# A causal mask taken from TensorE's accumulation to an add on VectorE, in the softmax heads of a decoder trunk

## The chip, the core and the metric

The kernel runs on one core of a Trainium2 chip. The metric is device time in microseconds, the median of several runs. The engines are named as the profile does: PE is TensorE's matmul and PEld its weight load, DVE is VectorE, ACT is ScalarE, POOL is GpSimd, SP is SyncE. Matmuls accumulate in PSUM, which has eight banks of 128 partitions by 512 float32 values; the other engines read the results from there.

## The reference

The program is a two-layer decoder trunk on 512 tokens of width 1024: an attention layer with an MLP, then a gated short convolution with an MLP. The attention layer has eight softmax heads with a forget gate ("forgetting attention") and eight stick-breaking heads, each 64 wide. The change is in the softmax heads alone:

```python
logits = jnp.einsum('bhqd,bhkd->bhqk', qi, k) * scale
logits = logits + fi[..., :, None] - cum_f[:, :, None, :]
causal = key_pos[None, :] <= q_pos[:, None]
logits = jnp.where(causal, logits, -jnp.inf)
p = jax.nn.softmax(logits, axis=-1)
return jnp.einsum('bhqk,bhkd->bhqd', p.astype(v.dtype), v)
```

For a block of 128 queries, keys of earlier blocks are all seen, keys of later blocks are not computed, and only the 128x128 block on the diagonal needs a mask.

## The kernel before

**Tiles.** Attention goes by pairs of heads `p`: 0 to 3 are softmax heads, 4 to 7 stick-breaking ones. The two heads of a pair are `e` = 0 and 1; they lie on different halves of the 128 partitions. Within a pair there are three units `u`: query blocks 0 and 1 together, block 2, block 3. One unit of one head fills one PSUM bank with scores: queries on the partitions, keys along the row. In u=0 the bank holds block 0 (one key block, at column 0) and block 1 (two key blocks, at column 256).

**A unit.** `logits(p, u)` makes the scores by products of float32 values split into a high and a low half (`q_hi`, `q_lo`, `k_hi`, `k_lo`): three matmuls per block and head, and in softmax heads a fourth for the forget gate (`dl`, `dr`), all at L688. Then come the mask products at L697: an identity in bf16 as weights and `mask` (0 on and below the diagonal, -1e30 above) as the moving side, which add the mask to the diagonal block. VectorE takes the negated maximum of a row (L705, `top`), ScalarE the exponential and its sum (L706, `w`, `total`), VectorE the reciprocal (L708, `inv`) and the scaling (L711).

**Around it.** `turn` transposes the weights of the unit before on TensorE (L748 for blocks 0 and 1, L760 for 2 and 3) into a `psc` bank, from where ScalarE copies the high half and VectorE subtracts the low half (`pt`, L754/L755 and L763/L764). `weigh` multiplies by the values (L784), whose halves VectorE adds up (L791). Between these, TensorE works off projections for later pairs: queries and keys (L313, L314, L315), values (L570 to L572), the sums of squares of the norm of queries and keys (L607, turned at L615, read by VectorE at L617), and the rows of that norm (L640, multiplied at L642, split at L415/L416). Weights of projections are halved by ScalarE (L292, `whi`) and VectorE (L293, `wlo`). Stick-breaking units have sigmoids (L726, L727) and a scan (L729) in place of maximum and exponential, and no mask product.

**PSUM.** Banks are handed out in three groups: `psa` (2), `psb` (4) and `psc` (2). Scores and projections take `psb`, so a unit's scores may have to wait until the exponentials of an earlier unit have read their bank. Transposes, sums of squares and rows take `psc`, so they wait until VectorE and ScalarE have read what stood there.

**The order.** The code is written in an order set by a counter, `spend` (L215): `logits`, `turn` and the projections each add an estimate in microseconds, and `fill` works off projections until a quota is used up. For a softmax unit the estimate at L681 has 0.12 per block for the mask. A scheduler then orders each engine's instructions once more when the program is built, except where `keep_in_program_order` holds them. Each engine runs its own list strictly in order, and waits on semaphores of the others.

## Time and profile before

| | |
|---|---|
| median of 3 runs | 1127.98 us (1127.93 to 1128.21) |
| the profiled execution | 1127.62 us |
| its span | 1125.3 us |
| PE busy | 1115.6 us, 99% of the span |
| PEld busy | 1009.8 us, 90% |
| DVE busy | 943.4 us, 84% |
| ACT busy | 679.9 us, 60% |
| mask products (L697) | 32, from 52.4 to 141.8 us |
| maxima (L705) | 32, from 52.7 to 143.3 us |

The span is from the first to the last instruction of the execution; what is left of its time lies around that. A matmul's duration in the profile includes its way through a pipeline, so that matmuls overlap: how long one holds TensorE is read from the start of one to the start of the next. The granted TensorE clock is 1.00 throughout the softmax stage. A row of the timeline gives start, length, engine, line, operation, `out<-in`, shapes and a count of equal instructions that follow each other; in brackets stands the idle time before it and what ended that. A row of waits gives total, times and longest. A row of instructions by group gives total busy time and the mean duration in ns of one.

### The profile page before, as it was taken

Reading aid. Unit: us, or ns where it says so; the run is one execution under the profiler, and the core shown is the slowest. Engines: PE = TensorE matmul, PEld = TensorE weight load, DVE = VectorE, ACT = ScalarE, POOL = GpSimd, SP = SyncE. Lnnn points to the kernel's source line nnn. Section 1 sums busy time; section 2 is a strip of 40 time slices with the busy share of each in tenths; the row PEclk is TensorE's granted clock in tenths of the full one; section 3 lists DMA queues with packets and bytes.
Section 4 is the critical chain, followed back from the end, with each engine's and each line's share of the span. In section 5 each row is a group of like instructions: output and inputs, shape, how many; then the busy total and the mean of one; then the engine's idle time right before and its main releaser. Section 6 shows DMA issues by size and latency. Waiting matters only on the chain.

```text
span 1125.3 us, 19407 instructions
## 1 busy us (share of the span) xinstructions
PE 1115.6 (99%) x7691; PEld 1009.8 (90%) x7691; DVE 943.4 (84%) x1439; ACT 679.9 (60%) x1013; POOL 158.6 (14%) x191
## 2 busy tenths in 40 slices
PE   9999999999999999999999999999999999999998
PEld 7888787878899999999999899988889999998886
DVE  6787888887899787888989889875799888898886
ACT  7556676655466766666557455543456766677553
POOL 4011111111101110014400001111111110014300
PEclk9999999999999999999999999999999999999999
DMA  6678777687877777799963455798887766699951
GB/s 194 173 180 200 179 180 200 155 205 206 197 208 201 208 192 197 206 277 205 228 173 77 120 153 125 157 229 216 207 208 188 177 174 159 183 265 195 233 153 57
DMA packets 175690, 209.34 MB, mean 186 GB/s; under 512 B 7564, under 2 KB 140220, under 8 KB 175600
## 3 DMA queue, kind: packets, MB, share of 16 engines
q0 software_dynamic: 41024, 86.95, 39.1%
q1 hardware_dynamic: 134416, 121.09, 34.8%
q8 instruction: 60, 0.98, 0.4%
q14 instruction: 30, 0.25, 0.1%
q10 hardware_dynamic: 160, 0.07, 0.0%
HBM read 203.10 MB, written 49.28 MB: 224 GB/s over the span
## 4 chain that ended last, share of the span: by engine, by line
PE 90%; DVE 4%; issue 2%; DMA 2%; ACT 1%; SPq 0%; DVEq 0%; ACTq 0%; POOLq 0%
PE psb L1056 25%; PE psb L1602 11%; PE psa L1056 10%; PE psa L1602 8%; PE psb L313 5%; PE psb L315 5%; PE psb L314 5%; PE psa L315 3%; PE psa L313 3%; PE psa L314 3%; PE psa L784 2%; PE psb L688 2%; DMA Xc<-in_conv_w_in 2%; PE psb L570 1%; PE psc L315 1%
## 5 line engine op out<-in xcount | busy, mean ns | idle before, releaser
L292 ACT ACTIVATE whi<-raw 128x1024 fp32r<-128x1024 f32 (+2 forms) x89 | 91.7, 1031 | 93.6 <-PE psb L314 29.9
L293 DVE TENSOR_TENSOR wlo<-raw,whi 128x1024 fp32r<-128x1024 f32 (+2 forms) x89 | 105.5, 1185 | 24.2 <-ACT whi L292 23.2
L1056 PE MATMUL psb<-p_lo,whi_p 128*128 128x256 f32 x432 | 121.7, 282 | 0.0
L1056 PE MATMUL psb<-p_hi,wlo_p 128*128 128x256 f32 x432 | 121.6, 281 | 0.0
L1056 PE MATMUL psb<-p_hi,whi_p 128*128 128x256 f32 x432 | 121.4, 281 | 0.0
L313 PE MATMUL psb<-hs_a,whi 128*128 128x512 f32 x224 | 92.2, 412 | 0.0
L315 PE MATMUL psb<-hs_a,wlo 128*128 128x512 f32 x224 | 88.7, 396 | 0.0
L1056 PEld LDWEIGHTS psb<-p_hi,whi_p 128*128 128x128 f32 x432 | 81.9, 190 | 0.0
L1056 PEld LDWEIGHTS psb<-p_lo,whi_p 128*128 128x128 f32 x432 | 81.4, 188 | 0.0
L1056 PE MATMUL psa<-p_hi,wlo_p 128*128 128x256 f32 x288 | 81.2, 282 | 0.0
L1056 PEld LDWEIGHTS psb<-p_hi,wlo_p 128*128 128x128 f32 x432 | 81.2, 188 | 0.0
L1056 PE MATMUL psb<-q_lo,whi_q 128*128 128x256 f32 x288 | 81.1, 282 | 0.0
L1056 PE MATMUL psa<-p_lo,whi_p 128*128 128x256 f32 x288 | 81.1, 282 | 0.0
L1056 PE MATMUL psb<-q_hi,wlo_q 128*128 128x256 f32 x288 | 81.1, 281 | 0.0
L1056 PE MATMUL psa<-p_hi,whi_p 128*128 128x256 f32 x288 | 80.9, 281 | 0.0
L1056 PE MATMUL psb<-q_hi,whi_q 128*128 128x256 f32 x288 | 80.9, 281 | 0.0
L1602 PE MATMUL psb<-act,whi 128*128 128x256 f32 x352 | 63.2, 282 | 0.0
L423 DVE SCALAR_TENSOR_TENSOR uv<-yv,taps,uv 128x511 f32<-128x511 f32 (+1 forms) x80 | 56.6, 744 | 0.0
L1602 PE MATMUL psb<-whi,act 128*128 128x512 f32 x176 | 56.4, 398 | 0.0
L423 DVE SCALAR_TENSOR_TENSOR ug<-yg,taps,ug 128x511 f32<-128x511 f32 (+1 forms) x80 | 55.5, 744 | 0.0
L1056 PEld LDWEIGHTS psa<-p_hi,whi_p 128*128 128x128 f32 x288 | 54.5, 189 | 0.1
L1056 PEld LDWEIGHTS psb<-q_hi,whi_q 128*128 128x128 f32 x288 | 54.6, 189 | 0.0
(478 smaller groups left out, 3619.3 us busy)
## 6 DMA issues: line engine op xcount, KB each, us to landing
t<-in_ffn_w_up POOLq DMA_DIRECT2D x42, 768.0 KB, 8.0
t<-t POOLq DMA_DIRECT2D x18, 768.0 KB, 5.5
raw<-in_attn_w_in SPq DMA_DIRECT2D x24, 512.0 KB, 5.3
X<-in_ffn_w_up SPq DMA_DIRECT2D x18, 512.0 KB, 5.1
Y<-t SPq DMA_DIRECT2D x18, 512.0 KB, 6.6
three<-t SPq DMA_DIRECT2D x18, 512.0 KB, 3.7
W<-in_ffn_w_up SPq DMA_DIRECT2D x18, 512.0 KB, 4.0
X<-in_ffn_w_up POOLq DMA_DIRECT2D x18, 512.0 KB, 8.0
```

The source lines that it names most:

```text
L292: return (act.activation(hi[:, at_], raw[:, at_], AF.Copy), dve.tensor_tensor(lo[:, at_], raw[:, at_], f32(hi[:, at_]), op=ALU.subtract))
L293: dve.tensor_tensor(lo[:, at_], raw[:, at_], f32(hi[:, at_]), op=ALU.subtract))
L313: made = [pe.matmul(acc, w[0], rhs[0], start=first, stop=False), pe.matmul(acc, w[0], rhs[1], start=False, stop=False), pe.matmul(acc, w[1 ...
L314: pe.matmul(acc, w[0], rhs[1], start=False, stop=False),
L315: pe.matmul(acc, w[1], rhs[0], start=False, stop=last)]
L423: dve.scalar_tensor_tensor(dst[:, d:], src[:, 0:S - d], tap(j), dst[:, d:], op0=ALU.mult, op1=ALU.add)
L570: pe.matmul(acc, lhs[0], w[0], start=first, stop=False)
L688: pe.matmul(ss[e][:, c:c + wide], ql[rows, b * P:n], kl[rows, 0:wide], start=first and b == bs[0], stop=last and b == bs[-1])
L784: pe.matmul(out_, w, t[:, first:first + step * (NB - k - 1) + 1:step, :], start=k == 0 and i == 0, stop=k == NB - 1 and i == 1)
L1056: pe.matmul(to, w[a][:, k, c], x[b][:, k, :], start=fresh and i + k + t == 0, stop=i == 1 and k == 3 and t == 2, skip_group_check=not fresh)
L1602: pe.matmul(to, l, r, start=begin and o + t == 0, stop=end and t == 2 and o == (0 if layer else 1), skip_group_check=not fresh)
```

## The change

The 32 mask products leave TensorE's accumulation, and the scores of the forget gate become the last of the group. Instead VectorE adds `mask` in place to the diagonal blocks in the score bank, just before the first maximum of each head of a unit. In u=0 one instruction takes both diagonal blocks of a bank (columns 0 and 384, 128x2x128), in u=1 and u=2 it takes one (128x128): six per pair, 24 in all. L681 and all else in the code stay as they are.

```diff
         scores(q_lo, k_hi, False, not fox)
         if fox:
-            scores(dl[:, p, :], dr, False, False)
-            for e in range(2):
-                for b, n, c, _ in parts:
-                    pe.matmul(ss[e][:, c + b * P:c + n], ident16, mask, start=False, stop=b == bs[-1])
+            scores(dl[:, p, :], dr, False, True)
...
             for j, (b, n, c, a) in enumerate(parts):
                 for e in range(2):
+                    if j == 0:
+                        diag = ss[e].rearrange("p (k q) -> p k q", q=P)[:, bs[0]:NB:3, :]
+                        dve.tensor_tensor(diag, diag, mask[:, None, :].to_broadcast([P, m, P]), op=ALU.add)
                     dve.reduce_max(top[:, j, e:e + 1], ss[e][:, c:c + n], axis=AX.X, negate=True)
```

In the changed file the add is at L704; the maximum stays at L705. The scheduler orders TensorE, VectorE and ScalarE anew around the softmax units. Behind the last of them the three lists are the same as before, and those of GpSimd and SyncE are the same throughout. Three places follow; the numbers in names are those of tiles and differ between the two programs.

TensorE at p=0, u=1 (two score banks, one per head; `psb_730` is a projection's). Before:

```order
L615 MATMUL psc_750<-ident,flat_759 128x128 x2
L688 MATMUL psb_806<-qk_hi_643,qk_hi_654 128x384
L688 MATMUL psb_806<-qk_lo_644,qk_hi_654 128x384
L688 MATMUL psb_807<-qk_hi_643,qk_hi_654 128x384
L688 MATMUL psb_807<-qk_lo_644,qk_hi_654 128x384
L688 MATMUL psb_806<-qk_hi_643,qk_lo_655 128x384
L688 MATMUL psb_807<-qk_hi_643,qk_lo_655 128x384
L688 MATMUL psb_806<-dr,dl 128x384
L688 MATMUL psb_807<-dr,dl 128x384
L697 LDWEIGHTS begin
L697 MATMUL psb_806<-mask,begin 128x128
```

And in the changed program:

```order
L615 MATMUL psc_750<-ident,flat_759 128x128 x2
L688 MATMUL psb_804<-qk_hi_643,qk_hi_654 128x384
L688 MATMUL psb_804<-qk_lo_644,qk_hi_654 128x384
L688 MATMUL psb_804<-qk_hi_643,qk_lo_655 128x384
L688 MATMUL psb_804<-dr,dl 128x384
L313 MATMUL psb_730<-hs_a_119,whi_618 128x512
L314 MATMUL psb_730<-hs_b_120,whi_618 128x512
L688 MATMUL psb_805<-qk_hi_643,qk_hi_654 128x384
L688 MATMUL psb_805<-qk_lo_644,qk_hi_654 128x384
L688 MATMUL psb_805<-qk_hi_643,qk_lo_655 128x384
L688 MATMUL psb_805<-dr,dl 128x384
```

The two heads' scores, mixed before, stand apart now, with two projection matmuls between them.

TensorE at p=1, u=0, where the sums of squares of a later pair (L607) meet the scores. Before:

```order
L572 MATMUL psb_989<-whi_881,hs_b_120 128x256
L688 MATMUL psb_1013<-qk_hi_948,qk_hi_959 128x256
L688 MATMUL psb_1014<-qk_hi_948,qk_hi_959 128x256
L688 MATMUL psb_1013<-qk_hi_948,qk_hi_959 128x256
L688 MATMUL psb_1014<-qk_hi_948,qk_hi_959 128x256
L688 MATMUL psb_1013<-qk_lo_949,qk_hi_959 128x256
L688 MATMUL psb_1014<-qk_lo_949,qk_hi_959 128x256
L607 MATMUL psc_1015<-sq_876,head_ones 32x128 x4
L607 MATMUL psc_1015<-sq_978,head_ones 32x128 x4
L688 MATMUL psb_1013<-qk_lo_949,qk_hi_959 128x256
```

And in the changed program:

```order
L572 MATMUL psb_987<-whi_879,hs_b_120 128x256
L607 MATMUL psc_1013<-sq_874,head_ones 32x128 x4
L607 MATMUL psc_1013<-sq_976,head_ones 32x128 x4
L688 MATMUL psb_1011<-qk_hi_946,qk_hi_957 128x256
L688 MATMUL psb_1012<-qk_hi_946,qk_hi_957 128x256
L688 MATMUL psb_1011<-qk_hi_946,qk_hi_957 128x256
```

The sums of squares stood inside the scores and now stand ahead of all of them.

VectorE at p=3, u=0, behind the split of a query tile (L655) and with the low halves of the transposed weights of p=2, u=2 (L764). Before:

```order
L655 SCALAR_TENSOR_TENSOR qk_lo_1729<-psb_1620,head_gains,qk_hi_1728 128x512
L293 TENSOR_TENSOR wlo_1736<-raw_1737,whi_1735 128x1024
L705 TENSOR_REDUCE top_1707<-psb_1684 128x1
L705 TENSOR_REDUCE top_1707<-psb_1685 128x1
L705 TENSOR_REDUCE top_1707<-psb_1684 128x1
L705 TENSOR_REDUCE top_1707<-psb_1685 128x1
L764 TENSOR_TENSOR pt_1532<-psc_1747,pt_1531 128x512
L708 RECIPROCAL inv_1709<-total_1708 128x4
```

And in the changed program:

```order
L655 SCALAR_TENSOR_TENSOR qk_lo_1721<-psb_1614,head_gains,qk_hi_1720 128x512
L704 TENSOR_TENSOR psb_1678<-psb_1678,mask 128x2x128
L704 TENSOR_TENSOR psb_1679<-psb_1679,mask 128x2x128
L705 TENSOR_REDUCE top_1697<-psb_1678 128x1
L705 TENSOR_REDUCE top_1697<-psb_1679 128x1
L293 TENSOR_TENSOR wlo_1728<-raw_1729,whi_1727 128x1024
L705 TENSOR_REDUCE top_1697<-psb_1678 128x1
L705 TENSOR_REDUCE top_1697<-psb_1679 128x1
L764 TENSOR_TENSOR pt_1526<-psc_1739,pt_1525 128x512
L764 TENSOR_TENSOR pt_1526<-psc_1746,pt_1525 128x512
```

The adds and the first maxima stand ahead of the halving of projection weights (L293), and the second L764 ahead of the reciprocal. On TensorE the sums of squares that follow there (L607, at 128.5 us in the profile before) stand three projection matmuls later than before.

## The prediction

> **What bounds the kernel now.** I read the page first: span, busy shares, chain that ended last.
>
> ```profile
> span 1125.3 us, 19407 instructions
> PE 1115.6 (99%) x7691; PEld 1009.8 (90%) x7691; DVE 943.4 (84%) x1439; ACT 679.9 (60%) x1013; POOL 158.6 (14%) x191
> PE 90%; DVE 4%; issue 2%; DMA 2%; ACT 1%; SPq 0%; DVEq 0%; ACTq 0%; POOLq 0%
> ```
>
> TensorE is the bound: 90% of the chain. So the unit of account is TensorE's time. What it saves in the softmax stage reaches the end unless a later wait eats it; what VectorE gains or loses counts only where TensorE waits for it. Next, the same by stretch, for the softmax heads (about 50 to 150 us), and the view of waits for TensorE:
>
> ```profile
> 50.00:100.00 50.00, 49.84 (x381) 41.48 (x380) 39.80 (x107) 30.88 (x75) 6.07 (x8) 1.00 0.80 187
> 100.00:150.00 50.00, 49.56 (x345) 39.74 (x344) 39.76 (x103) 31.69 (x67) 6.54 (x9) 1.00 0.75 183
> PE psc L607 <- DVE pt L764: 1.1, 2, 0.7
> ```
>
> The columns are window, length, then busy time of PE, PEld, DVE, ACT, POOL. VectorE is busy 79.6 of these 100 us, so it has 20 us of room, but a wait that TensorE has is for VectorE (L764, which frees a `psc` bank). Work moves from the full engine to the second fullest.
>
> **Removed: 32 mask products.** Their own duration (219 ns by the view of the tile) is a pipelined latency, so I price them by start times: from the last scores to the second full matmul behind them, in a softmax unit with masks and in a stick-breaking unit, which has none. First u=0 (four masks), then u=1 (two).
>
> ```profile
> 97.44 0.40 PE L688 MATMUL psb<-dr,dl 64*128 64x256 f32 x4
> 97.77 0.40 PE L697 MATMUL psb<-mask,begin 128*128 128x128 bf16 x4
> 97.98 0.48 PE L313 MATMUL psb<-hs_a,whi 128*128 128x512 f32 x1
> 98.29 0.40 PE L314 MATMUL psb<-hs_a,whi 128*128 128x512 f32 x1
> ...
> 172.80 0.40 PE L688 MATMUL psb<-qk_hi,qk_lo 64*128 64x256 f32 x4
> ...
> 173.47 0.40 PE L314 MATMUL psb<-hs_a,whi 128*128 128x512 f32 x1
> ```
>
> ```profile
> 104.52 0.33 PE L688 MATMUL psb<-dr,dl 64*128 64x384 f32 x2
> 104.78 0.28 PE L697 MATMUL psb<-mask,begin 128*128 128x128 bf16 x2
> 104.88 0.48 PE L313 MATMUL psb<-hs_a,whi 128*128 128x512 f32 x1
> 105.19 0.39 PE L314 MATMUL psb<-hs_a,whi 128*128 128x512 f32 x1
> ...
> 179.53 0.34 PE L688 MATMUL psb<-qk_hi,qk_lo 64*128 64x384 f32 x2
> ...
> 180.13 0.39 PE L314 MATMUL psb<-hs_a,whi 128*128 128x512 f32 x1
> ```
>
> 0.85 - 0.67 = 0.18 us for four masks, 0.67 - 0.60 = 0.07 for two; u=2 has two as well. Four pairs: 4 x (0.18 + 0.07 + 0.07) = **1.3 us saved**.
>
> The weight loads could be what counts instead:
>
> ```profile
> L697 PEld LDWEIGHTS <-begin 128*128 128x128 bf16 x32 | 1.8, 97 | 3.0 <-issue 2.4
> ```
>
> 32 x 97 ns = 3.1 us if none of it were hidden; but four masks start within 0.21 us (97.77 to 97.98), so most of it is hidden. [...]
>
> **Added: 24 adds on VectorE**, 8 of 128x256 and 16 of 128x128, PSUM to PSUM. No instruction of VectorE writes PSUM in this trace, so I bound the cost by neighbours:
>
> ```profile
> L705 DVE TENSOR_REDUCE top<-psb 128x1 f32<-128x128 f32 x8 | 1.9, 285 | 3.8 <-PE psb L697 3.8
> L755 DVE TENSOR_TENSOR pt<-psc,pt 128x256 fp32r<-128x256 f32 x4 | 1.7, 422 | 0.1
> L729 DVE TENSOR_TENSOR_SCAN rest<-rest,begin 128x256 f32<-128x256 f32 x8 | 5.2, 676 | 0.0
> L729 DVE TENSOR_TENSOR_SCAN rest<-rest,begin 128x128 f32<-128x128 f32 x8 | 3.0, 408 | 1.2 <-ACT rest L726 1.2
> 52.71 0.49 DVE L705 TENSOR_REDUCE top<-psb 128x1 f32<-128x128 f32 x2 [1.83 <-PE psb L697]
> ```
>
> Low end 422 and 285 ns, high end 676 and 408 (the scan). I take the low end, since L755 too combines a PSUM tile and an SBUF tile element by element, while a scan carries a value along. Two reductions of 285 in 0.49 us start 0.20 apart, so an engine slot is some 0.08 shorter than a duration: 0.34 and 0.20. In all 8 x 0.34 + 16 x 0.20 = 6.0 us of VectorE, 0.7 per u=0 unit and 0.4 per other. It fits the 20 us of room. In front of the maximum, each exponential comes 0.3 to 0.5 us later. The four score banks (`psb`) come free with the exponentials, and the transposes of a unit follow in the next round (a unit takes some 7 us: 96.63 to 103.89 below); neither is close, except at the first place.
>
> **Moved, first place (p=0, u=1, 54.4 us).** e=1's scores wait for the bank of e=0 of u=0, so for its second exponential. The new order puts e=0's four scores, two projection matmuls, then e=1's four. Two heads' scores use different rows and run side by side; a single head takes as long as the pair.
>
> ```profile
> 54.38 0.70 PE L688 MATMUL psb<-qk_hi,qk_hi 64*128 64x384 f32 x2
> ...
> 55.94 0.39 PE L314 MATMUL psb<-hs_b,whi 128*128 128x512 f32 x1
> 56.17 0.40 PE L315 MATMUL psb<-hs_a,wlo 128*128 128x512 f32 x1
> 57.79 0.38 PE L748 MATMUL psc<-ident,w 128*128 128x128 f32 x2
> ...
> 103.89 0.44 PE L688 MATMUL psb<-qk_hi,qk_hi 64*128 64x384 f32 x2
> ...
> 55.29 0.48 DVE L711 TENSOR_SCALAR w<-w,inv 128x128 f32<-128x128 f32 x2
> ```
>
> Now: 55.94 - 54.38, less 0.23 for the projection in it, is 1.33, 1.26 without masks. Then: twice 0.89 (103.89 to 104.78) plus 0.08 behind each group (0.31 against 0.23) and 0.1 to re-enter, 2.04. **0.8 us lost.** VectorE's second add waits here for e=1's scores until 56.6, with the scalings (L711) of u=0 queued behind it: 1.4 us later than the 55.29 of now, and done in under 1 us (four in two times 0.48), by 57.7. TensorE's transposes of them (L748), at 57.79 now, come some 0.6 later then: no wait. The next unit's adds wait for TensorE anyway, where VectorE idles now.
>
> **Second place (p=1, u=0, 69.6 us).** Now the sums of squares (L607) cut the scores in two and wait for L764; then they stand ahead of all sixteen scores.
>
> ```profile
> 69.61 0.50 PE L688 MATMUL psb<-qk_hi,qk_hi 64*128 64x256 f32 x4
> ...
> 72.09 0.28 PE L571 MATMUL psb<-wlo,hs_a 128*128 128x256 f32 x1
> ...
> 96.63 0.50 PE L688 MATMUL psb<-qk_hi,qk_hi 64*128 64x256 f32 x4
> ...
> 147.56 0.65 PE L607 MATMUL psc<-sq,head_ones 128*32 128x128 f32 x16
> 148.13 0.50 PE L688 MATMUL psb<-qk_hi,qk_hi 64*128 64x256 f32 x4
> ```
>
> 2.48 now, 2.36 without the L570 in it. Then 0.57 for the block, 1.14 for the scores (96.63 to 97.77), 0.1 behind: 1.81. Of the 0.55 the masks are 0.18, so **0.4 us gained**. VectorE's L293 moves behind both L764 here, so the bank is free in time.
>
> **Third place (p=3, u=0, 128.5 us).** TensorE stands 0.6 us before L607:
>
> ```profile
> 127.67 0.40 PE L315 MATMUL psb<-hs_a,wlo 128*128 128x512 f32 x1
> 128.51 0.64 PE L607 MATMUL psc<-sq,head_ones 128*32 128x128 f32 x16 [0.44 <-DVE pt L764]
> ```
>
> 0.84 instead of 0.23. Then three more projections (0.7 us) come first, and on VectorE adds and first maxima stand before L293, with L764 right behind the maxima: **0.6 us gained**.
>
> **Given back.** Two other waits for `psc` (67 and 120.7 us), where TensorE arrives as VectorE ends: 0.1 each, an estimate. And at 151.5:
>
> ```profile
> 148.33 0.39 ACT L610 ACTIVATE flat<-psc 128x256 f32<-128x256 f32 x1 [0.19 <-PE psc L607]
> ...
> 150.43 0.42 DVE L729 TENSOR_TENSOR_SCAN rest<-rest,begin 128x128 f32<-128x128 f32 x1 [1.15 <-ACT rest L726]
> 151.34 0.17 DVE L617 SCALAR_TENSOR_TENSOR qv<-psc,least 128x16 f32<-128x16 f32 x1 [0.50 <-PE psc L615]
> ```
>
> TensorE comes 1.3 us early (the terms up to here). VectorE, some 1.0 early when the last pair's u=1 begins, loses 0.4 to each unit's adds and is hardly 0.2 early at the last exponentials; ScalarE works on from them to L610 with 0.19 us of idle time, so L729 is early by 0.2 to 0.3 and L617, right behind it, by 0.7 (151.34 to 150.65): **0.6 us lost**. Behind it VectorE waits for TensorE and ScalarE again, and the later stages hold nothing of this change.
>
> **Sum**: -1.3 + 0.8 - 0.4 - 0.6 + 0.2 + 0.6 = -0.7 us. The profiled run took 1127.62 (span 1125.3 and 2.3 around it), 0.36 under the median: 1126.9 on that run, **1127.3** against the median of 1127.98. Less than 0.2% (2.3 us, about what a measurement of this kernel tells from no change).
>
> **Rivals.** *The adds land on TensorE*: VectorE becomes the pace of the softmax stage, TensorE waiting for L642, L755 and L764 at the half dozen places where it arrives just as they end (66, 70, 74, 87, 120, 128 us). For it: 6.0 us on an engine 80% busy, up to 11.9 if an add costs a scan. Against it: VectorE's idle stretches in front of most units (1.83 us at 52.71). It decides once 3.6 of the 6.0 us arrive (3.6 - 1.3 = 2.3); at three quarters it is 4.5 - 1.3 = +3.2, 1131.2, and all of it 1132.7. [...]
> *The pairing loss does not come and both stalls go*: e=1's scores slip in beside other work: -1.3 - 0.4 - 0.6 = -2.3 and a little, 1125.6.
> *The loads count*: 3.1 us for the masks and the other terms (+0.6): 1125.5.
>
> **How the numbers follow.** Forecast (1126.0 to 1128.8) 0.55; adds on TensorE 0.25; no pairing loss 0.15; loads 0.05. Same 0.55, faster 0.20, slower 0.25. The range goes from 1125.2, below both faster rivals, to 1131.0, about the middle of the slower one, which leaves out some 0.15.
>
> **What would show it.** In the changed kernel's profile: 24 adds at 285 and 422 ns; L688 at 54 us in two groups half a microsecond apart; L607 at 70 us in one piece; no wait at 128.5; a wait for L617 near 151. TensorE's first matmul behind the masks' places 0.18 or 0.07 sooner. I am wrong if TensorE gets new waits for VectorE between 60 and 130 us, if adds take over 600 ns, or if time moves behind 260 us.

## The result

| kernel | median of runs (us) | ratio to before, 95% interval |
|---|---|---|
| before | 1128.15 (22 runs, 1126.91 to 1130.11) | |
| after | 1126.62 (22 runs, 1125.18 to 1127.97) | 0.9981 [0.9975, 0.9987] |

The change saves 1.5 us, 0.19%. The forecast was 0.7 us saved. Most of this part is about why a total inside the forecast's range was put together in another way, and where the other 0.8 us are.

The page of the kernel after: span, busy shares, and the chain that ended last.

```profile
span 1123.0 us, 19372 instructions
PE 1113.5 (99%) x7659; PEld 1008.7 (90%) x7659; DVE 948.2 (84%) x1463; ACT 679.7 (61%) x1013; POOL 158.1 (14%) x191
PE 96%; DVE 3%; ACT 1%; issue 0%; DVEq 0%; ACTq 0%
```

TensorE is still the bound, with 32 matmuls fewer; VectorE has 24 instructions more. The softmax stretch by windows (columns as in the prediction):

```profile
50.00:100.00 50.00, 49.40 (x356) 40.62 (x355) 42.23 (x119) 30.25 (x71) 5.88 (x8) 1.00 0.75 179
100.00:150.00 50.00, 50.00 (x340) 40.38 (x339) 42.06 (x116) 33.12 (x75) 6.44 (x9) 1.00 0.76 182
```

The adds, from the groups by form:

```profile
L704 DVE TENSOR_TENSOR psb<-psb,mask 128x128 f32<-128x128 f32 x16 | 4.1, 292 | 0.7 <-PE psb L688 0.7
L704 DVE TENSOR_TENSOR psb<-psb,mask 128x256 f32<-128x256 f32 x8 | 3.0, 427 | 2.1 <-PE psb L688 2.0
```

The waits of TensorE between 45 and 156 us:

```profile
PE psb L688 <- ACT w L706: 0.6, 1, 0.6
```

VectorE went from 79.6 to 84.3 us of these 100 (+4.7, forecast 6.0). The adds take 292 and 427 ns (forecast 285 and 422), and what they wait for is TensorE. The one wait that TensorE has left in this stretch is new, and it is for ScalarE: 0.6 us in front of L688, at the first place.

**Where the time went.** Most matmuls of two kernels are the same instructions in the same order, so I match them and subtract their start times. The table gives that difference to the kernel before, each column set to zero at 45 us, just ahead of the first score (each number is the middle one of some six neighbouring matmuls; the kernel before, profiled a second time, stays within 0.05 of zero throughout).

| at (us of before) | behind what | after | after, second profile |
|---|---|---|---|
| 53 | masks of p=0, u=0 | -0.18 | -0.18 |
| 57 | first place | +1.22 | +1.21 |
| 66 | unit u=2 | +1.16 | +1.15 |
| 73 | second place | +0.64 | +0.61 |
| 98 | p=1 and p=2, u=0 | +0.32 | +0.26 |
| 126 | p=2, p=3 u=0 | -0.02 | -0.09 |
| 131 | third place | -0.53 | -0.60 |
| 143 | p=3 | -0.69 | -0.78 |
| 258 | end of attention | -0.64 | -0.71 |

The softmax stage gives -0.64 to -0.71, the -0.7 of the forecast. It is not the same sum: the first place cost more, and the loss at 151.5 us didn't come. Behind 258 us two more steps follow, at 711 to 715 and near 1103 us, of which the forecast had nothing. All were tested; the cause of the last one stays open.

### The profile page after: what moved, and what is told of

The parts are those of the page before. It is cut to its first block, busy times and chain, and to the rows that moved or that the text cites. A ratio compares the mean times of both kernels' runs of the same rounds, so it can differ in the third digit from the quotient of the medians.

```text
span 1123.0 us, 19372 instructions
## 1 busy us (share of the span) xinstructions
PE 1113.5 (99%) x7659; PEld 1008.7 (90%) x7659; DVE 948.2 (84%) x1463; ACT 679.7 (61%) x1013; POOL 158.1 (14%) x191
## 4 chain that ended last, share of the span: by engine, by line
PE 96%; DVE 3%; ACT 1%; issue 0%; DVEq 0%; ACTq 0%
PE psb L1056 28%; PE psa L1056 11%; PE psb L1602 11%; PE psa L1602 8%; PE psb L313 6%; PE psb L315 5%; PE psb L314 5%; PE psa L315 3%; PE psa L313 3%; PE psa L314 3%; PE psb L688 2%; PE psa L784 2%; PE psb L570 1%; PE psc L760 1%; PE psb L571 1%; PE psb L572 1%
## 5 line engine op out<-in xcount | busy, mean ns | idle before, releaser
L293 DVE TENSOR_TENSOR wlo<-raw,whi 128x1024 fp32r<-128x1024 f32 (+2 forms) x89 | 105.6, 1186 | 23.5 <-ACT whi L292 23.0
L1056 PE MATMUL psb<-p_lo,whi_p 128*128 128x256 f32 x432 | 121.8, 282 | 0.0
L1056 PE MATMUL psb<-p_hi,wlo_p 128*128 128x256 f32 x432 | 121.7, 282 | 0.0
L1056 PE MATMUL psb<-p_hi,whi_p 128*128 128x256 f32 x432 | 121.4, 281 | 0.0
L1056 PEld LDWEIGHTS psb<-p_hi,whi_p 128*128 128x128 f32 x432 | 82.0, 190 | 0.0
L1056 PEld LDWEIGHTS psb<-p_lo,whi_p 128*128 128x128 f32 x432 | 81.4, 188 | 0.0
L1056 PEld LDWEIGHTS psb<-p_hi,wlo_p 128*128 128x128 f32 x432 | 81.4, 188 | 0.0
L1056 PE MATMUL psa<-p_hi,wlo_p 128*128 128x256 f32 x288 | 81.3, 282 | 0.0
L1056 PE MATMUL psb<-q_lo,whi_q 128*128 128x256 f32 x288 | 81.1, 282 | 0.0
L1056 PE MATMUL psb<-q_hi,wlo_q 128*128 128x256 f32 x288 | 81.1, 282 | 0.0
L1056 PE MATMUL psa<-p_lo,whi_p 128*128 128x256 f32 x288 | 81.1, 282 | 0.0
L1056 PE MATMUL psa<-p_hi,whi_p 128*128 128x256 f32 x288 | 80.9, 281 | 0.0
L1056 PE MATMUL psb<-q_hi,whi_q 128*128 128x256 f32 x288 | 80.9, 281 | 0.0
L1056 PEld LDWEIGHTS psa<-p_hi,whi_p 128*128 128x128 f32 x288 | 54.6, 190 | 0.1
L1602 PEld LDWEIGHTS psb<-act,whi 128*128 128x128 f32 x352 | 54.2, 189 | 0.5 <-DVE act L1006 0.3
```

The source lines that it names most:

```text
L293: dve.tensor_tensor(lo[:, at_], raw[:, at_], f32(hi[:, at_]), op=ALU.subtract))
L1056: pe.matmul(to, w[a][:, k, c], x[b][:, k, :], start=fresh and i + k + t == 0, stop=i == 1 and k == 3 and t == 2, skip_group_check=not fresh)
L1602: pe.matmul(to, l, r, start=begin and o + t == 0, stop=end and t == 2 and o == (0 if layer else 1), skip_group_check=not fresh)
```

## The experiments

Beside each experiment the kernel before ran on the same chip (medians 1128.10 to 1128.32), and ratios are to that. Code is shown against the changed kernel unless another is named.

### Both kernels again: what repeats

> The kernel before, unchanged, as a second profile beside the next ones. Two readings of the 1.5 us between the two medians are open: the softmax stage alone (-0.70 us of matmul start times between 45 and 150 us) or a further 0.8 us that the change causes behind 260 us, where the changed kernel's matmuls started a little earlier with every 100 us (-0.42 at 218 us, -2.4 at 1103 us). If that drift is between runs and not of the change, two profiles of this one kernel drift against each other by up to 2 us behind 260 us too, with no step between 45 and 150 us; if it is of the change, the two agree within 0.3 us at every place. Time: the same as before, within 0.05%.

Measured: 1127.92 us, ratio 0.9999 [0.9988, 1.0009]; no step anywhere in the softmax stage, and the start (0.3 us later in the first 20 us) is the only difference until 711 us, where it stalls 0.14 us less.

> The changed kernel, unchanged, as a second profile. If the drift behind 260 us is of the change, this profile drifts against a profile of the kernel before by the same 2 us behind 260 us as the first did; if it is between runs, the drift differs in size or sign, while the steps in the softmax stage (+1.3 to +1.4 at 56 us, -0.57 at 72 us with masks, -0.7 at 128 us) come back within 0.1 us. Time: 0.13 to 0.2% below the kernel before.

Measured: 1126.14 us, 0.9979 [0.9971, 0.9988], 2.0 us below before. The steps of the softmax stage came back within 0.1 us (second column of the table). The slow drift between 370 and 600 us did not: the first profile of the changed kernel gains 0.85 us there on the kernel before, the second nothing. In the first, neighbouring 128x256 matmuls start 118.3 ns apart on average between 370 and 600 us, in the second and in both profiles of before 118.8 ns. Two of the experiments below, no mask and VectorE's order held, also stand at 118.3, the other kernels without a moved tile at 118.8. So this drift is between runs and not of the change; what sets the two levels stays open. What does repeat is a step of about -0.6 us at 711 to 722 us and one of -0.25 us near 1103 us against the first profile of before.

### No mask at all, and masks by matmul in the first unit alone

```diff
-                    if j == 0:
-                        diag = ss[e].rearrange("p (k q) -> p k q", q=P)[:, bs[0]:NB:3, :]
-                        dve.tensor_tensor(diag, diag, mask[:, None, :].to_broadcast([P, m, P]), op=ALU.add)
```

> No causal mask for the softmax heads at all: neither matmuls nor adds (that part of the computation is left out). TensorE's order at p=0, u=1 stays as in the kernel before (the two heads' scores mixed), L607 stands ahead of the scores at p=1, u=0, and L607 near 128 us stays where it was. Theory (masks -1.3, first place only where the pair is split, second place -0.4, the wait at 128.5 caused by VectorE and so perhaps shorter): -1.7 to -2.3 us against the kernel before, about 0.6 to 0.9 below the changed kernel. Rival, adds land on TensorE by some 2 us in the changed kernel: this one would then be 2 us or more below the changed kernel, with waits of TensorE for VectorE gone between 60 and 130 us. Rival, the loads count: -3.1 and more.

Measured: 1125.16 us, 0.9972 [0.9960, 0.9984]. The softmax stage is at -1.71 against before (45 to 258 us), 1.0 below the changed kernel. Behind the first place the two stand 1.28 apart (-0.06 against +1.22), and from there on the changed kernel makes up 0.2 to 0.3: taking the adds away altogether brings nothing at the other places. The rival that adds land on TensorE by 2 us, and the one that the weight loads count 3.1 us, are both out.

```diff
-            scores(dl[:, p, :], dr, False, True)
+            scores(dl[:, p, :], dr, False, p + u > 0)
+            for e in range(2 if p + u == 0 else 0): [pe.matmul(ss[e][:, c + b * P:c + n], ident16, mask, start=False, stop=b == bs[-1]) for b, n, c, _ in parts]
...
-                    if j == 0:
+                    if j == 0 and p + u > 0:
```

> Hybrid: the masks of the first unit (p=0, u=0) by matmul as before, all other masks by VectorE's add. TensorE's order at p=0, u=1 is then mixed as before, while L607 stands ahead of the scores at p=1, u=0 and behind more projections near 128 us, as in the changed kernel. Theory: the first place costs the changed kernel 1.3 to 1.4 us, so this one gains masks -1.1, second place -0.4, third place -0.6 or -0.7: -2.1 us against the kernel before, 1.2 us below the changed kernel. Rival (the later waits simply take the place of the first: the 1.4 us at 56 us is slack that TensorE would lose again at 67 to 74 us): within 0.4 us of the changed kernel, with new waits for VectorE at L607 or L764 between 60 and 75 us.

Measured: 1125.66 us, 0.9971 [0.9960, 0.9982], 2.5 us below before and 0.5 below the changed kernel beside it (1126.14), where 1.2 below was expected. The traces do have the 1.2 in the softmax stage; the single runs of the two kernels overlap (1124.31 to 1125.92 and 1124.82 to 1127.80). The stage is at -1.91 (forecast -2.1), with -0.06 behind the first place, -0.64 behind the second, -1.80 behind the third, and next to no loss between 143 and 258 us (-1.98 to -1.91). So the loss of the first place is a real price and nothing later would have eaten it. It also settles the wait for L617 at 151.5 us: here TensorE comes 2 us early, more than the 1.3 that I had reckoned with, and still doesn't wait.

### The first place: what the 1.4 us are

The forecast had 0.8 us: two heads' scores one after the other. ScalarE's timeline explains the rest. First the kernel before, then the changed kernel (the load of the table for exponentials, and the first exponential):

```profile
51.38 0.39 ACT L610 ACTIVATE flat<-psc 128x256 f32<-128x256 f32 x1 [0.83 <-PE psc L607]
51.78 1.28 ACT L706 ACT_TABLE_LOAD   x1
53.08 0.37 ACT L706 ACTIVATE w<-psb,top 128x128 f32<-128x128 f32 x1
```

```profile
51.62 0.38 ACT L610 ACTIVATE flat<-psc 128x256 f32<-128x256 f32 x1 [0.83 <-PE psc L607]
53.76 1.28 ACT L706 ACT_TABLE_LOAD   x1 [1.76 <-DVE top L705]
55.06 0.37 ACT L706 ACTIVATE w<-psb,top 128x128 f32<-128x128 f32 x1
```

Before, the table was loaded while VectorE looked for the first maximum, and cost nothing. After, the load itself waits for the maximum. The built order shows why (ScalarE, the first softmax unit, before and after):

```
50 L706 ACT_TABLE_LOAD
51 L706 ACTIVATE w_781,total_783<-psb_748,top_782 128x128 [waits DVE_49]
```

```
50 L706 ACT_TABLE_LOAD [waits DVE_49]
51 L706 ACTIVATE w_777,total_779<-psb_748,top_778 128x128 [waits PE_49]
```

With the add in between, VectorE's maximum waits only for VectorE's add, so the exponential has to wait for TensorE's scores by itself, beside VectorE's maximum: two waits, and the first of them stands ahead of the table load. The exponentials start 1.98 us later (53.08 to 55.06). 0.24 of it is a later start of the stage, 0.46 are the two adds less the masks, 1.28 is the table. TensorE, which needs the bank that the second exponential frees, stands still:

```profile
55.07 0.33 PE L688 MATMUL psb<-dr,dl 64*128 64x384 f32 x1
55.34 0.50 PE L313 MATMUL psb<-hs_a,whi 128*128 128x512 f32 x1
55.68 0.40 PE L314 MATMUL psb<-hs_b,whi 128*128 128x512 f32 x1
56.62 0.44 PE L688 MATMUL psb<-qk_hi,qk_hi 64*128 64x384 f32 x1 [0.55 <-ACT w L706]
```

The test: one small exponential early, so that the table is loaded there. No engine's order changes otherwise, but a tile more is reserved (see the 20 us below).

```diff
-            m = len(bs)
+            m = len(bs); p + u or act.activation(tiny.tile([P, 1], F32, tag="early", name="early", bufs=1), f32(q_hi[:, 0:1]), AF.Exp, scale=0.0)
```

> The changed kernel with one small exponential (128x1) for ScalarE right behind the first pair's L415, so that ScalarE loads its table for exponentials there, some 6 us before the first maximum, and not behind it; no other engine's order changes. Open: why the loss at the first place came out at 1.3 to 1.4 us and not 0.8. Theory: in the changed kernel the first exponential depends on two engines (VectorE's maximum and TensorE's scores), and the table load (1.28 us) stands behind the wait for VectorE, where in the kernel before it ran while VectorE still worked: the first exponential starts 1.98 us later, not 0.67. With the load out of the way the wait of TensorE for the bank (0.55 us, ended by ScalarE) is gone, and the first place costs 0.7 us (the split alone): the softmax stage between 45 and 258 us at about -1.3 against before, 0.6 below the changed kernel. Rival (the adds alone make the exponentials late): the wait stays and the stage is within 0.15 us of the changed kernel's -0.65.

Measured in the trace: the first exponential at 54.05 follows the maximum at once, and TensorE has no wait left between 45 and 156 us (ScalarE's timeline, then TensorE's):

```profile
51.90 0.38 ACT L610 ACTIVATE flat<-psc 128x256 f32<-128x256 f32 x1 [0.83 <-PE psc L607]
54.05 0.37 ACT L706 ACTIVATE w<-psb,top 128x128 f32<-128x128 f32 x1 [1.77 <-DVE top L705]
```

```profile
55.95 0.39 PE L314 MATMUL psb<-hs_b,whi 128*128 128x512 f32 x1
56.26 0.44 PE L688 MATMUL psb<-qk_hi,qk_hi 64*128 64x384 f32 x1
```

The first place costs +0.75 net of its two masks, instead of +1.40, and the stage is at -1.43 (forecast -1.3). Adding the 0.07 of the masks, the split alone is 0.82 and the table load made the other 0.65. That part of the theory stands.

The load takes 1.28 us in both traces, and in both the exponential starts 0.02 us behind its end (51.78 + 1.28 against 53.08 before, 53.76 + 1.28 against 55.06 after).

But the time was 1106.23 us, 0.9801 [0.9788, 0.9815]: 22 us below the kernel before and 20 below the changed one, where 0.6 below the changed one was expected. That is taken up further down.

### VectorE's order, and VectorE's load

```diff
-                        dve.tensor_tensor(diag, diag, mask[:, None, :].to_broadcast([P, m, P]), op=ALU.add)
-                    dve.reduce_max(top[:, j, e:e + 1], ss[e][:, c:c + n], axis=AX.X, negate=True)
+                        pin(dve.tensor_tensor(diag, diag, mask[:, None, :].to_broadcast([P, m, P]), op=ALU.add))
+                    pin(dve.reduce_max(top[:, j, e:e + 1], ss[e][:, c:c + n], axis=AX.X, negate=True))
```

> The changed kernel with adds and first maxima held in the order of the program on VectorE (add of head 0, its maximum, add of head 1, its maximum) at every unit. The order of TensorE: e=0's scores at p=0, u=1 are still a group of their own, and L607 near 128 us stands where it stood in the kernel before. Theory: at the first place the wait for ScalarE's exponential (0.7 us of the 1.3 us lost) gets shorter by an add, 0.2 to 0.3 us, and the split itself stays, so +1.0 to +1.2 there; the third place's wait comes back (+0.6). Together the softmax stage at 0 to -0.3 against before. Rival (the whole loss at the first place is the wait, not the split): +0.6 or less at the first place.

Measured: 1125.45 us, 0.9977 [0.9967, 0.9987]; the stage at -0.91, better than expected. The first place: +1.20 net, with a wait of 0.4 us (an add less than the changed kernel), as expected. The third place was the miss: L607 stands where it stood before, yet the 0.5 us are gained too, because in this order VectorE comes to L764 earlier, at 126.71 us (127.77 in the profile before; VectorE's timeline, then TensorE's):

```profile
126.71 0.69 DVE L764 TENSOR_TENSOR pt<-psc,pt 128x512 fp32r<-128x512 f32 x1
```

```profile
127.47 0.40 PE L315 MATMUL psb<-hs_a,wlo 128*128 128x512 f32 x1
127.81 0.65 PE L607 MATMUL psc<-sq,head_ones 128*32 128x128 f32 x16
```

With the early exponential beside it:

> The kernel with adds and maxima in program order on VectorE, with the early exponential too. Theory: the wait of TensorE at the first place (0.36 us there) goes, the split of the pair stays: the softmax stage at about -1.3 to -1.4 against before, where the one without the early exponential had -0.91. Rival (the wait was caused by the adds): unchanged, -0.9.

Measured: the stage at -1.36 (forecast -1.3 to -1.4) and the first place at +0.75 net, as in the other kernel with the early exponential; the wait is gone. 1106.62 us, 0.9811 [0.9795, 0.9826].

```diff
                         dve.tensor_tensor(diag, diag, mask[:, None, :].to_broadcast([P, m, P]), op=ALU.add)
+                        dve.tensor_tensor(diag, diag, mask[:, None, :].to_broadcast([P, m, P]), op=ALU.add)
```

> The changed kernel with every add made twice (the mask is added twice; the weights that it leaves at zero stay zero): 24 adds, 6 to 7 us of VectorE more in the softmax stage, whose share rises from 84 to about 90 of 100 us. TensorE has e=1's scores at p=0, u=1 still further back, behind all six projections. Theory (adds are hidden in VectorE's idle time in front of each unit; what costs TensorE is where its order is cut): within -0.5 to +1.0 us of the changed kernel between 45 and 258 us, no new wait above 0.3 us but at the first place. Rival (adds land on TensorE as soon as VectorE has no room): +3 to +6 us, spread over the units at 60 to 130 us.

Measured: 1127.55 us, 0.9994 [0.9985, 1.0003]; the stage at +0.07, so 24 adds more cost 0.7 to 0.8 us and not 3 to 6. Windows and the only wait of TensorE in the stage:

```profile
50.00:100.00 50.00, 49.61 (x355) 40.84 (x354) 44.40 (x132) 29.96 (x69) 5.88 (x8) 1.00 0.80 191
100.00:150.00 50.00, 49.98 (x336) 39.85 (x335) 43.90 (x128) 32.84 (x73) 6.61 (x9) 1.00 0.77 189
```

```profile
PE psb L688 <- ACT w L706: 0.3, 1, 0.3
```

VectorE is at 88.3 of 100 us and TensorE still waits for it nowhere here. The 0.7 us are again a matter of order: at the third place L607 was moved into the scores (none of the 0.5 us is gained there).

The hybrid with VectorE's order held:

```diff
-            scores(dl[:, p, :], dr, False, True)
+            scores(dl[:, p, :], dr, False, p + u > 0)
+            for e in range(2 if p + u == 0 else 0): [pe.matmul(ss[e][:, c + b * P:c + n], ident16, mask, start=False, stop=b == bs[-1]) for b, n, c, _ in parts]
...
-                    if j == 0:
+                    if j == 0 and p + u > 0:
...
-                        dve.tensor_tensor(diag, diag, mask[:, None, :].to_broadcast([P, m, P]), op=ALU.add)
-                    dve.reduce_max(top[:, j, e:e + 1], ss[e][:, c:c + n], axis=AX.X, negate=True)
+                        pin(dve.tensor_tensor(diag, diag, mask[:, None, :].to_broadcast([P, m, P]), op=ALU.add))
+                    pin(dve.reduce_max(top[:, j, e:e + 1], ss[e][:, c:c + n], axis=AX.X, negate=True))
```

> The hybrid (first unit's masks by matmul, so that its table load waits for nothing and the two heads' scores at p=0, u=1 stay mixed) with adds and maxima of the other units in program order on VectorE. Theory: first place free as in the hybrid, so -1.9 in the softmax stage as there, and another 0.2 to 0.3 from the order on VectorE (the changed kernel gained that much by it): -2.1 to -2.2, and the shorter code stream takes 0.4 to 0.6 at 711 to 715 us: some 2.5 to 2.8 us below the kernel before. Rival (the order on VectorE gained only by the shorter wait at the first place): -1.9, the same as the hybrid.

Measured: 1124.72 us, 0.9972 [0.9962, 0.9982]. -1.95 at 143 us, as the hybrid without it (-1.98), so the rival holds up to there and the forecast of -2.1 to -2.2 fails; then 0.4 us are lost between 155 and 215 us, where TensorE's one wait for L764 in front of L640 is 1.7 us and not 1.3 as in both kernels:

```profile
PE psc L640 <- DVE pt L764: 1.7, 1, 1.7
```

The median lies 3.6 us below the kernel before, where 2.5 to 2.8 were expected, but the profiled execution took 1126.40 us, 1.7 above that median. Four of the nine runs lie at 1125.8 to 1126.4 and five at 1124.2 to 1124.7; what sets these two levels is open, and the trace shows the upper one alone.

### 711 to 715 us: where TensorE's own code is fetched

The waits of TensorE's weight loads between 700 and 720 us in the kernel before (the changed kernel has none there):

```profile
PEld psb L1056 <- ACT Xsc L1108: 0.3, 1, 0.3
PEld psb L1056 <- DVE wlo_q4c L1006: 0.2, 1, 0.2
```

All four stalls of TensorE there, by start times, are 0.57 us in one profile of before and 0.43 in the other. By the order of the waits they come from a weight transfer of the convolution stage (Xc, issued by POOL at L1083) that lands late; its chunks follow one another in a ring, and the delay arrives at TensorE two chunks later. What differs is when TensorE's code is fetched. The rows of DMA queues show packets of 16 KB (q8, `instruction`); counted against TensorE's matmuls and weight loads there is one for each 256 on average (60 packets, 15,382 of them; in the changed kernel 60 and 15,318), and by this count I take them for TensorE's code. With 64 instructions fewer in the softmax stage, the 53 packets behind 143 us start 3.5 us later on average in the changed kernel (-0.5 to +8.5), 50 of them later than before.

```diff
     # the kernel before, start-up
-    for _ in range(WARM):
+    for k in range(WARM - 32):
         pe.matmul(t[:, 0:P], blank, blank, start=True, stop=True)
```

> The kernel before with 2 warm-up matmuls in place of 34 at its start: 32 matmuls and 32 weight loads fewer, as many as the change took away, but none of them in the softmax heads. Theory (code fetch): the stalls of TensorE at 711 to 715 us and near 1103 us vanish, so -0.4 to -0.6 and -0.2 us there; no step between 45 and 258 us. The start-up may lose time (first matmuls at a lower clock) or not: 0 to +3 us, read from the first 20 us. Rival (the stalls hang on the softmax stage's time): both stay as in the kernel before.

```diff
     # the changed kernel, start-up
-    for _ in range(WARM):
-        pe.matmul(t[:, 0:P], blank, blank, start=True, stop=True)
+    for k in range(WARM + 32):
+        n = P if k < WARM else 8
+        pe.matmul(t[0:n, 0:n], blank[:, 0:n], blank[:, 0:n], start=True, stop=True)
```

> The changed kernel with 32 small matmuls (8x8, on zeros, into an unused bank) more at the start-up, behind the warm-up matmuls, so that TensorE's instruction stream behind the softmax heads stands at the same place as in the kernel before (32 matmuls and 32 weight loads had gone). Open: both profiles of the kernel before have four stalls of TensorE at 711 to 715 us (0.43 and 0.57 us in all) and two more near 1103 us (0.2 us); no changed kernel so far has the first, and three of four lack the second. Theory (TensorE's own code fetch, 16 KB every 256 instructions, fell at 667.7 us into the transfer of Xc between 661.9 and 672.9 us and made it 0.75 us longer, which reaches TensorE at 711 us; in the changed kernels it falls 3.8 us later against TensorE): with the 64 instructions put back, the stalls at 711 to 715 us (0.4 to 0.6 us) and those near 1103 us (0.2 us) come back, while the softmax stage stays at -0.65 against before between 45 and 258 us. Time: the changed kernel's + 0.7, and what the 32 matmuls cost at the start (0 to 2 us, read from the first 20 us). Rival (the stalls hang on when TensorE gets there, 1 to 2 us earlier or later, not on the fetch): no stalls, as in the other changed kernels.

Measured: the kernel before with 32 matmuls fewer at its start (1128.27 us, 0.9999 [0.9990, 1.0008]; it starts 1.35 us later) has no step in the softmax stage and no stall at 711 us: -0.54 there. The changed kernel with 32 more (1127.79 us, 0.9996 [0.9987, 1.0005]; it starts 1.85 us later) keeps its -0.69 in the softmax stage and has the stalls, larger than before: 1.2 us here, and 1.3 more between 640 and 704 us. This profile is of its longest execution, 1130.35 us and 2.6 above its median; the granted clock was 0.50 from 7.6 to 11.0 us in it, which is part of the late start (the first two projections start 0.52 us apart there, 0.33 in the kernel before). So the size of the stalls in it need not be the usual one, and the median neither confirms nor excludes them. Its waits between 700 and 720 us, and then the code packet among the DMA queues (count, MB, share) from the issue of Xc to its cast (663.04 to 674.59):

```profile
PEld psb L1056 <- ACT Xsc L1108: 0.9, 1, 0.9
PEld psb L1056 <- DVE wlo_q4c L1006: 0.2, 1, 0.2
```

```profile
q8 instruction: 1, 0.02, 1.1%
```

| kernel | Xc, issue to the start of its cast (us) | code packet, us after the issue | stalls 704 to 724 us |
|---|---|---|---|
| before, two profiles | 11.03, 11.38 | 5.8, 5.5 | 0.57, 0.43 |
| after, 32 matmuls more | 11.55 | 5.3 | 1.22 |
| after, two profiles | 10.25, 10.15 | 9.6, 9.5 | 0, 0 |
| before, 32 matmuls fewer | 10.16 | 10.5 | 0 |
| no mask; hybrid; two adds; pinned; hybrid pinned | 10.34, 10.22, 10.18, 10.12, 10.13 | 9.6, 9.5, 9.6, 10.7, 9.3 | 0 each |
| early exponential; the same pinned; hybrid pinned with the tile of the next section | 10.21, 10.12, 10.00 | 9.4, 10.8, 10.3 | 1.55, 1.08, 1.20 (at 698 to 703 us) |

In the first eleven profiles the stalls went with the number of TensorE's instructions ahead, and the two tests turned them off and on, with one profile each. That this happens by the packet falling into the middle of the transfer fits these eleven, but the packet alone was not moved. The last three profiles show that it is not the only way: there the same matmuls stall although the packet comes late and the transfer is as short as without stalls. TensorE, whose matmuls follow each other faster in these three kernels (113 to 114 ns apart, next section), gets there 47 us after the issue of Xc and not 49. So the stalls depend on how late the weights come against TensorE, and the number of instructions ahead is one thing that moves this.

The step near 1103 us is another matter. Two stalls of 0.1 us each, ended by nothing that the profile shows, stand in five profiles (both of before, before with 32 fewer, the hybrid, two adds) and not in six (both of after, no mask, after with 32 more, pinned, hybrid pinned). Both tests had expected them to follow the number of instructions, and they did not; their cause is open.

### The 20 us: 32 bytes

In both kernels with the early exponential the softmax stage gained what was expected, and then they gained 20 us behind 258 us. Their 128x256 matmuls start 113 ns apart in place of 118 to 119. Beside the table load one thing differs: the small tile for the exponential's result shifts 577 later tiles by 32 bytes in SBUF. So the last run reserves the tile and uses it for nothing, in the hybrid with VectorE's order held:

```diff
     # the hybrid with VectorE's order held
-            m = len(bs)
+            m = len(bs); p + u or tiny.tile([P, 1], F32, tag="early", name="early", bufs=1)
```

> The hybrid with adds and maxima in program order, and beside it one tile of 128x1 reserved in the pool of small tiles and used by nothing: no engine's instructions change, but 577 later tiles lie 32 bytes further in SBUF (among them the stationary operands of the convolution and FFN stages, from 64 to 96 bytes past a multiple of 128, the moving weights staying at 32). Open: the two kernels with the early exponential gained 20 us behind 258 us, where the pitch of a 128x256 matmul fell from 118 or 119 to 113 ns; their early exponential reserved such a tile too. Theory A (the place in SBUF sets the pitch): pitch 113 ns here too, and 1104 to 1106 us, some 20 us below the hybrid without the tile. Theory B (the early table load on ScalarE, or a passing condition of the chip in that call, made the matmuls faster): pitch 118 to 119 ns and 1124 to 1126 us as without the tile.

Measured: 1105.75 us, 0.9804 [0.9791, 0.9817], 19 us below the same instructions without it (1124.72). Windows of the stretch from 370 to 600 us, without the tile and with it:

```profile
370.00:600.00 230.00, 230.00 (x1937) 229.82 (x1936) 194.53 (x248) 147.29 (x198) 39.33 (x35) 1.00 0.81 205
```

```profile
370.00:600.00 230.00, 228.20 (x1999) 227.17 (x1998) 201.08 (x259) 151.19 (x205) 39.31 (x35) 1.00 0.81 205
```

62 matmuls more in the same time, at the same granted clock (1.00). Theory A holds: the place in SBUF sets the pitch. At L1056 ten 128x256 matmuls take 1.14 us by their starts with the tile (499.76 to 500.90, 114 ns each) and 27 take 3.18 us without it (999.74 to 1002.92, 118 ns each). The expectation names the operands the wrong way round: the tiles that moved (activations and convolution inputs, 0 to 32 bytes past a multiple of 64) are the moving operands of these matmuls, and the weights, the stationary ones, stay at 32. By the addresses in the built programs, some 5,100 of the changed kernel's matmuls have their operands at 0 and 32 past a multiple of 64 (the kernel without the tile has them there too); with the tile, some 7,000 have both at 32. Whether it is the moving operand's own place or the distance of the two that counts was not tried, nor the tile in the kernel before. It has nothing to do with the mask. The tile changes the softmax stage by less than 0.1 us (-1.62 against -1.53 at 258 us), so what the kernels with the early exponential show of the first place stands.

This kernel and the two with the early exponential (1106.23 and 1106.62 us) are about 2% below the kernel before and 1.8% below the changed one.

## Why the prediction was right, and where it was wrong

Taken by its own steps, against the kernel before:

| step | forecast | measured |
|---|---|---|
| 32 masks off TensorE | -1.3 | -1.3 |
| first place | +0.8 | +1.5 (0.8 split, 0.65 table load) |
| second place | -0.4 | -0.35 |
| third place | -0.6 | -0.5 |
| two waits for `psc` | +0.2 | 0 |
| wait for L617 | +0.6 | 0 |
| softmax stage | -0.7 | -0.65 |
| behind 260 us | 0 | -0.45 to -0.6 at 711 us, -0.2 near 1103 us |

**Masks: right.** Pricing by start times held, pricing by weight loads (3.1 us) did not. Last scores and the next full matmuls, first u=0, then u=1:

```profile
98.20 0.40 PE L688 MATMUL psb<-dr,dl 64*128 64x256 f32 x4
98.53 0.50 PE L313 MATMUL psb<-hs_a,whi 128*128 128x512 f32 x1
98.86 0.39 PE L314 MATMUL psb<-hs_a,whi 128*128 128x512 f32 x1
...
105.10 0.33 PE L688 MATMUL psb<-dr,dl 64*128 64x384 f32 x2
105.36 0.50 PE L313 MATMUL psb<-hs_a,whi 128*128 128x512 f32 x1
105.69 0.39 PE L314 MATMUL psb<-hs_a,whi 128*128 128x512 f32 x1
```

0.66 (before 0.85) and 0.59 (before 0.67). The -1.3 of the table is the sum of the steps that the matched matmuls show at these places.

**Adds: right.** 24 of them, hidden, at the durations of their nearest neighbours. The rival that had 0.25 of the chance, VectorE as the pace of the stage, is refuted even at twice the load. Of the two waits of L607 for L764 that the prediction had shown as a sign of a tight VectorE, one alone is in the softmax stage (0.44 us at 128.5); the other, 0.66 us, is at 205 us.

**First place: mechanism right, size wrong.** L688 did come in two groups, and the split cost the 0.8 us: a head's four scores alone take 0.90 us in the changed kernel (54.44 to 55.34), where the pair together takes 0.89 in the kernel before (103.89 to 104.78). What failed is the sentence "In front of the maximum, each exponential comes 0.3 to 0.5 us later": the first came 1.98 us later (0.24 of it from the later start of the whole stage), since I looked at the order of ScalarE's instructions and not at which of them carry the waits. The table load's row was in the profile of before, and its new wait in the built order. So the two groups of L688 stood 1.28 us apart (55.34 to 56.62) and not the half microsecond that I had given as a sign.

**Second place: right.** L607 in one piece ahead of the scores, 72.97 - 71.04 = 1.93 from its start to the second projection behind them, against 2.48 before:

```profile
71.04 0.64 PE L607 MATMUL psc<-sq,head_ones 128*32 128x128 f32 x16
71.61 0.50 PE L688 MATMUL psb<-qk_hi,qk_hi 64*128 64x256 f32 x4
72.42 0.40 PE L688 MATMUL psb<-dr,dl 64*128 64x256 f32 x4
72.75 0.39 PE L570 MATMUL psb<-whi,hs_a 128*128 128x256 f32 x1
72.97 0.28 PE L571 MATMUL psb<-wlo,hs_a 128*128 128x256 f32 x1
```

**Third place: right.** No wait before L607 (0.33 behind the last projection, 0.84 before), with the first of VectorE's two L764 done in time (VectorE's timeline, then TensorE's):

```profile
128.06 1.28 DVE L764 TENSOR_TENSOR pt<-psc,pt 128x512 fp32r<-128x512 f32 x2
```

```profile
128.59 0.40 PE L315 MATMUL psb<-hs_a,wlo 128*128 128x512 f32 x1
128.92 0.65 PE L607 MATMUL psc<-sq,head_ones 128*32 128x128 f32 x16
```

The later place of L607 was not needed for it: with no mask, and with VectorE's order held, L607 stands where it stood and the 0.5 us are gained too, by an earlier L764.

**Given back at 151.5 us: wrong.** I had ScalarE fall behind with the adds and be early by only 0.2 to 0.3 us. It was early by as much as TensorE (ScalarE's timeline, then VectorE's):

```profile
147.50 0.51 ACT L563 ACTIVATE v<-psb,ncol_n 128x256 fp32r<-128x256 f32 x1
147.88 0.40 ACT L610 ACTIVATE flat<-psc 128x256 f32<-128x256 f32 x1
```

```profile
150.90 0.17 DVE L617 SCALAR_TENSOR_TENSOR qv<-psc,least 128x16 f32<-128x16 f32 x1 [0.48 <-PE psc L615]
```

L610 comes at 147.88 (before 148.33) and L617 at 150.90 (before 151.34), 0.45 and 0.44 earlier, or 0.7 against the start of the stage, which is 0.24 later in this profile; TensorE is 0.7 early too, and L617 still waits for it. The hybrid, with TensorE 2 us early and no loss here, shows that the term is zero and not only small. It cancelled the error at the first place: the stage's sum was right to 0.1 us because +0.7 there met -0.6 here and -0.2 at the two waits for `psc`, which did not come either. That is luck.

**"the later stages hold nothing of this change": wrong.** The prediction had named time that moves behind 260 us as a sign of being wrong, and it did. By the two tests of the code fetch the change's instruction count is worth about 0.5 us at 711 us; 0.2 us more, near 1103 us, are of unknown cause. With them the traces give -1.3 to -1.5, and the medians -1.5 and -2.0. So the forecast of the whole, -0.7, was about half of what was measured.

## What to carry to other kernels

A change that gives an operand a second writer can give its readers a second wait; look where that wait is put, above all when the instruction ahead is a table load that ran for nothing until now (here 1.28 us). Price a removed instruction by start times (here 1.3 us, where its weight loads last 3.1), and check the sum place by place: two wrong terms can hide in a right total. And before reading any difference of a per cent or two as the work of a change, compare the pitch of identical matmuls far away from it: the addresses of tiles (here 32 bytes, 19 us) and the number of instructions ahead (here 64, about 0.5 us) both reached there.

## What the runs showed of the hardware that was not expected

- The same 128x256 matmuls start 113 to 114 ns or 118 to 119 ns apart, by 32 bytes in SBUF: 19 us of 1125.
- Packets of 16 KB, by their count TensorE's code, come one for each 256 of its matmuls and weight loads on average (60 for 15,382). A packet in the middle of a 512 KB weight transfer went with 11.0 to 11.6 us from issue to cast, against 10.0 to 10.3 us.
- A table load of 1.28 us came to stand behind a wait of the exponential that follows it, and went from hidden to exposed.
- An add in place on a PSUM tile takes 292 ns (128x128) and 427 ns (128x256), two in a row 0.76 us for the wider: about what a maximum of 128x128 (285 ns) and a subtraction of 128x256 into SBUF (422 ns) take.
- Two profiles of one kernel can differ by 0.45 ns in the pitch of the same matmuls (118.3 and 118.8), 0.85 us over 230; the cause is open.
